# A hybrid SSM and attention layer on one core: both heads' scores in one PSUM tile of two banks

## The chip, the core and the metric

The kernel runs on one core of a Trainium2 chip. The metric is the device time of one launch in microseconds (us), as the median of the runs shown. TensorE is called PE here, VectorE DVE, ScalarE ACT, GpSimd POOL and SyncE SP, as in the profile.

## The reference, cut to what matters

One layer of a decoder with two branches, on 1024 prompt tokens and 32 sample tokens (8 sequences of 4), 1056 tokens in all. Both branches read one projection of the normalised input, and their gated sum and a feed-forward part are added to the stream:

```python
z = _rmsnorm(x, p['norm1_g']) @ p['w_in']
q, k, v, u, g = jnp.split(z, [o1, o2, o3, o4], axis=-1)     # q 512, k 128, v 128, u 512, g 2048
q = _rmsnorm(q.reshape(b, t, N_HEADS, HEAD_DIM), p['q_norm_g'])      # 8 heads of 64, 2 kv heads
k = _rmsnorm(k.reshape(b, t, N_KV_HEADS, HEAD_DIM), p['k_norm_g'])
attn, k_state, v_state = attn_fn(q, k, v, p['attn_sinks'])  # window of 128 keys, ALiBi, sinks
ssm, h_re, h_im = _s5_branch(u, h0_re, h0_im, p)            # scan over time, GELU, then y * sigmoid(y @ w_glu + b)
mixed = g_attn * (attn @ p['w_attn_o']) + g_ssm * (ssm @ p['w_ssm_o'])
x = x + mixed @ p['w_out']
hdn = jax.nn.relu(_rmsnorm(x, p['norm2_g']) @ p['w_up'])
x = x + (hdn * hdn) @ p['w_down']
```

## The kernel before

The activations lie with features on the partitions and the 1056 tokens along the free axis, cut into three chunks of 352 columns (c = 0, 1, 2). A dense product in fp32 is made of three fp32r matmuls (high part by high part, low by high, high by low: L131 to L133), each 128x128 by 352 columns. The weights come by DMA as `wraw` and are split into `whi` (ACT, L117) and `wlo` (DVE, L118).

The program runs in phases: the projection to `u`; the SSM in four quarters q (`stage0` to `stage3`), while PE takes the other projections (`z`) between; the norm of queries and keys; attention in eight blocks b of 128 queries, while PE takes the gates' projections (`z`) and then the GLU (`glu`) and the first of the output projections (`so`, `ao`) between; then the second phase with `so`, `ao`, `wo`, and last the feed-forward part, which the change doesn't reach. The order of instructions on each engine isn't written by hand: a scheduler lays it out from priorities, dependencies and free buffers, except where `in_turn` or `follow` adds an order. On the chip each engine takes its instructions in that order and waits at the first one that isn't ready.

PSUM has eight banks of 128x512 fp32, handed out by the tags `mm` (three), `sa` (two), `sb` (two) and `sc` (one). In the first phase `mmt`, `msa`, `msb` and `msc` give tiles of one bank each. With `msa` come: the first two chunks of the second tile of `u` (L329); the SSM's inputs `pv`, real and imaginary part, in two halves hb per quarter (L602), which four multiplications on DVE (L612 to L615) and two copies on ACT (L616, L617) read; the sums of squares of queries and keys (L726); the attention scores `sc` (L809); and the scores of the sample tokens `ssc` (L873). In the second phase `mmt2` (L972) goes through a cycle of seven tiles, of which the second and the sixth have the tag `sa`.

`attn_scores` makes the scores of a block in two parts mp of four matmuls: two query tiles m by two heads h. A head has 64 features, so a matmul uses one half of the rows (heads h = 1 and 0 use different halves), 128 queries by 256 keys (128 in block 0); head h writes to bank h. DVE adds the bias and takes the maximum out of PSUM (L820), ACT takes the exponential (L827), DVE scales (L835), PE transposes (`pt`, L841), ACT copies (`ptt`, L844), and PE makes the product with the values (`po`, L851). `sa_read` and `in_turn` give PE's scores an order: one after the other, and after the last read of the scores before.

The low parts of the squares of queries and keys, `qsl` (L731), come from the pool T2, of which three buffers exist, which the gates' tiles use as well. The tag `ptb` of the attention pool has two buffers of 128x1152, used only by the sample tokens, later.

The first products of the GLU read `a_hi` and `a_lo`, the split outputs `gr` of the SSM (`split`, L934: a cast on ACT, L935, and a subtraction on DVE, L936). `gemm_c` goes through the inputs k for one chunk; `gemm_k` goes through the chunks for one input, and so needs three banks at a time.

Of the kernel before, what the change touches and what calls it, by code (L numbers as in the profile page):

```python
# [23 lines left out]
CH = T // 3  # L24
# [34 lines left out]
def trunk_kernel(ctx, tc, xt, wts, wff, pp_d, cp_d, g1_d, abias, sbias, ckt, cvr, ck_tail, cv_tail,  # L59
# [142 lines left out]
    with ExitStack() as ph1:  # L202
# [3 lines left out]

        def msa(name):
            return pp1.tile([P, 512], F32, tag="sa", bufs=2, name=name)

# [3 lines left out]
        def msc(name):  # L213
            return pp1.tile([P, 512], F32, tag="sc", bufs=1, name=name)
# [70 lines left out]
        with phs:  # L285
# [42 lines left out]
            u0 = [mmt(f"u0_{c}") for c in range(3)]  # L328
            u1 = [msa("u1_0"), msa("u1_1"), msc("u1_2")]  # L329
            for k in range(8):  # L330
# [263 lines left out]
            def stage2(q, ut, s1o):  # L594
# [6 lines left out]
                for hb in range(2):  # L601
                    pv = [msa(f"pv{q}{hb}{ri}") for ri in range(2)]  # L602
                    for j in range(2):
# [121 lines left out]
        A.copy(bonr, C("bones"))  # L725
        pqs = [msa("qkss0"), msa("qkss1"), msc("qkss2")]  # L726
        for t_ in (4, 0, 1, 2, 3):
            z = kt if t_ == 4 else q4[:, t_, :]
            sq = newT(f"qsq{t_}")
            sqh = ap_.tile([P, 2048], F32R, tag="st", bufs=2, name=f"qsh{t_}")[:, :T]  # L730
            sql = newT2(f"qsl{t_}", F32R)  # L731
            A.activation(sq, z, AF.Square)
            A.copy(sqh, sq)
            V.tensor_sub(sql, sq, sqh.bitcast(F32))
            w = bonr[:, 8 - 2 * t_ : 18 - 2 * t_]
            for c in range(3):
                mm_(pqs[c][:10, :CH], w, sqh[:, chunks[c]], start=(t_ == 4), stop=False)
                mm_(pqs[c][:10, :CH], w, sql[:, chunks[c]], start=False, stop=(t_ == 3))
# [51 lines left out]
        def sink_terms(mx, sk, n, name):  # L790
# [5 lines left out]
            return nm, es  # L796
        sa_read = []


        def attn_scores(b):  # L800
# [6 lines left out]
            for mp in range(2):  # L807
                mms = []
                pst = [msa(f"sc{b}{mp}{h}") for h in range(2)]  # L809
                for m2 in range(2):  # L810
                    m = 2 * mp + m2
                    for h in (1, 0):
                        hs_ = slice(64 * h, 64 * h + 64)
                        mms.append(mm_(pst[h][:, m2 * 256 : m2 * 256 + nk], q4[hs_, m, b * P : b * P + P],
                                       kt[hs_, k0 : k0 + nk], start=True, stop=True))
                in_turn(mms, *sa_read)
                for m2 in range(2):
                    for h in range(2):
                        hd = 4 * h + 2 * mp + m2
                        rd = V.tensor_tensor_reduce(  # L820
                            st[:, hd, :nk], pst[h][:, m2 * 256 : m2 * 256 + nk], ab[:, hd, bo : bo + nk],
                            1.0, C("sink", hd, hd + 1), ALU.add, ALU.max, mx[:, hd : hd + 1],
                        )
                sa_read[:] = [rd.ins.name]
            nm, es = sink_terms(mx, C("sink"), NH, f"{b}")
# [30 lines left out]
        def attn_sample():  # L856
# [10 lines left out]
            mxs = [ap_.tile([P, 3], F32, tag="smx", bufs=2, name=f"smx{h}") for h in range(2)]  # L867
            ptbs = [ap_.tile([P, 9, P], F32, tag="ptb", bufs=2, name=f"ptb{h}") for h in range(2)]
            for h in range(2):
                nc.sync.dma_start(sbs[h], sbias[h])  # L870
            for c in range(3):
                s = chunks[c]
                pst = [msa(f"ssc{h}{c}") for h in range(2)]  # L873
                mms = []
                for h in (1, 0):
                    hs_ = halves[h]
                    mms.append(mm_(pst[h][:, :CH], qs[hs_, :, :].rearrange("p m t -> p (m t)"), kall[hs_, s],
                                   start=True, stop=True))
                in_turn(mms, *sa_read)
                for h in range(2):  # L880
                    mx = mxs[h]
                    rd = V.tensor_tensor_reduce(
                        ssts[h][:, s], pst[h][:, :CH], sbs[h][:, s], 1.0,
                        C("ssink", h, h + 1) if c == 0 else mx[:, c - 1 : c], ALU.add, ALU.max, mx[:, c : c + 1],
                    )
                sa_read[:] = [rd.ins.name]
            for h in range(2):
# [63 lines left out]
        for m in range(4):  # L951
# [3 lines left out]
            nc.sync.dma_start(gr, y_d[m])  # L955
            th = newT2(f"gth{m}")
            for c in range(3):
                ps = mmt(f"glu{m}_{c}")
                gemm_c([blk(wg, (m % 2) * 4 + k) for k in range(4)], aacts, ps, c)
                A.activation(th[:, chunks[c]], ps[:, :CH], AF.Tanh, bias=bh[:, 16 + m : 17 + m], scale=0.25)  # L960
# [7 lines left out]
    with ExitStack() as ph2:  # L968
        accp = ph2.enter_context(tc.tile_pool(name="accp", bufs=1))
        _mi = [0]  # L970

        def mmt2(name):  # L972
            i = _mi[0]
            _mi[0] += 1
            tag, n = (("mm", 3), ("sa", 2), ("mm", 3), ("sb", 2), ("mm", 3), ("sa", 2), ("sb", 2))[i % 7]
            return pp1.tile([P, 512], F32, tag=tag, bufs=n, name=name)

# [561 lines left out]
```

## Time and profile before

| what | us |
|---|---|
| three runs of the kernel before | 1361.0, 1364.49, 1365.66 |
| median | 1364.49 |
| the profiled execution | 1364.98 |
| its span, first to last instruction | 1363.2 |
| PE busy in it | 1311.4 (96%) |
| DVE, ACT, POOL busy | 906.5, 513.1, 484.8 |
| mean granted clock of PE | 0.987 |

A busy time of an engine is the time in which at least one of its instructions runs. A timeline gives for each instruction, or group of like ones in a row, its start, its duration and the idle time of its engine before it with what ended that; "x2" counts records, and a score in fp32 leaves two of them per matmul, a dense fp32r matmul one. Durations of PE's matmuls overlap, so what one costs is read from its start to the start of the next.

### The profile page before, as it was taken

What the parts mean: (1) busy time and instruction counts of PE and PEld (TensorE: products, weight loads), DVE (VectorE), ACT (ScalarE), POOL (GpSimd) and SP (SyncE); (2) the same over time, 40 slices, a digit from 0 to 9 for tenths busy, and PEclk for the clock granted to TensorE, in tenths of its full rate; (3) what the DMA queues carried; (4) which work ended last, traced back from release to release, by engine and by line L of the source; (5) the groups of instructions that cost most, each with busy time, mean ns of one, the idle gap of its engine ahead of it and who ended that gap; (6) DMA issues with size and microseconds to landing.
All of it is one profiled execution on the core that took longest, in us unless ns stands there. A gap on an engine that the chain in (4) does not pass through costs nothing.

```text
span 1363.2 us, 23526 instructions
## 1 busy us (share of the span) xinstructions
PE 1311.4 (96%) x9405; PEld 1250.7 (92%) x9405; DVE 906.5 (67%) x1383; ACT 513.1 (38%) x857; POOL 484.8 (36%) x356
## 2 busy tenths in 40 slices
PE   7988999999998999999999999999998999999998
PEld 6987999899876777999989999999998999999898
DVE  7859675534457856654686666566598595887973
ACT  5111233234147544223453444344365362533420
POOL 5495522000000000004344665675675332343630
PEclk9889999999998999999999999999999999999999
DMA  7233434463233313524233564444467382563621
GB/s 266 84 85 79 103 99 95 116 242 105 65 95 95 114 62 115 203 82 162 102 110 111 190 190 138 143 155 143 143 198 238 112 263 75 152 202 115 220 95 64
DMA packets 91789, 184.96 MB, mean 136 GB/s; under 512 B 23616, under 2 KB 32832, under 8 KB 91392
## 3 DMA queue, kind: packets, MB, share of 16 engines
q1 hardware_dynamic: 84768, 170.48, 39.6%
q10 hardware_dynamic: 6912, 12.98, 2.5%
q8 instruction: 74, 1.21, 0.4%
q14 instruction: 35, 0.29, 0.1%
HBM read 125.70 MB, written 57.56 MB: 134 GB/s over the span
## 4 chain that ended last, share of the span: by engine, by line
PE 74%; DVE 8%; DMA 3%; issue 2%; ACT 2%; POOL 1%; SPq 0%; DVEq 0%; POOLq 0%; ACTq 0%
PE X L1150 6%; PE X L1151 6%; PE X L1152 6%; PE C L1151 4%; PE z L131 4%; PE C L1150 4%; PE C L1152 4%; PE z L133 4%; PE z L132 4%; PE wo L131 2%; PE wo L132 2%; PE wo L133 2%; PE D L1151 2%; PE Y L1151 2%; PE D L1150 2%
## 5 line engine op out<-in xcount | busy, mean ns | idle before, releaser
L1150 PE MATMUL X<-slot_hi,fw 128*128 128x264 f32 x768 | 218.5, 285 | 2.0 <-ACT h L1169 0.9
L1151 PE MATMUL X<-slot_lo,fw 128*128 128x264 f32 x768 | 217.8, 284 | 0.4 <-DVE slot_lo L1076 0.4
L1152 PE MATMUL X<-slot_hi,fw 128*128 128x264 f32 x768 | 217.6, 283 | 0.0
L131 PE MATMUL z<-x_hi,whi 128*128 128x352 f32 x528 | 174.2, 330 | 1.8 <-DVE zt L268 1.8
L133 PE MATMUL z<-x_hi,wlo 128*128 128x352 f32 x528 | 172.9, 328 | 1.5 <-DVE wlo L118 1.5
L132 PE MATMUL z<-x_lo,whi 128*128 128x352 f32 x528 | 172.9, 328 | 0.0
L1012 DVE TENSOR_TENSOR fw<-f,fw 128x512 fp32r<-128x512 f32 x128 | 132.4, 1035 | 35.1 <-ACT fw L1011 35.1
L1150 PEld LDWEIGHTS X<-slot_hi,fw 128*128 128x128 f32 x768 | 144.6, 188 | 3.0 <-ACT h L1169 1.4
L1151 PEld LDWEIGHTS X<-slot_lo,fw 128*128 128x128 f32 x768 | 144.7, 188 | 0.6 <-DVE slot_lo L1076 0.6
L1152 PEld LDWEIGHTS X<-slot_hi,fw 128*128 128x128 f32 x768 | 144.1, 188 | 0.0
L1111 POOL TENSOR_TENSOR q<-x 128x528 f32<-128x528 f32 x4 | 5.7, 1432 | 374.2 <-DVE x L1102 374.2
L1011 ACT CAST fw<-f 128x512 fp32r<-128x512 f32 x128 | 79.2, 619 | 155.8 <-PE Y L1152 61.8
L997 POOL TENSOR_TENSOR f_s<-f,f 128x512 f32<-128x512 f32 x32 | 49.5, 1546 | 216.6 <-DMA f<-in_dram 176.2
L1012 DVE TENSOR_TENSOR fw<-f_s,fw 128x512 fp32r<-128x512 f32 x96 | 92.9, 969 | 38.3 <-ACT fw L1011 38.1
L133 PEld LDWEIGHTS z<-x_hi,wlo 128*128 128x128 f32 x528 | 100.0, 189 | 5.7 <-issue 3.6
L131 PEld LDWEIGHTS z<-x_hi,whi 128*128 128x128 f32 x528 | 100.6, 190 | 4.6 <-ACT whi L117 2.1
L132 PEld LDWEIGHTS z<-x_lo,whi 128*128 128x128 f32 x528 | 100.6, 191 | 2.0 <-issue 1.5
L117 ACT CAST whi<-wraw 128x1024 fp32r<-128x1024 f32 (+3 forms) x46 | 46.5, 1012 | 144.8 <-PE z L132 74.1
L1011 ACT CAST fw<-f_s 128x512 fp32r<-128x512 f32 x96 | 59.9, 624 | 90.0 <-PE C L1152 48.2
L1150 PE MATMUL Y<-slot_b,fw 128*128 128x264 f32 x256 | 73.3, 287 | 5.4 <-DVE y L1169 2.8
L1150 PE MATMUL C<-slot_b,fw 128*128 128x264 f32 x256 | 72.8, 285 | 0.9 <-ACT slot_b L1306 0.5
L1151 PE MATMUL C<-slot_b,fw 128*128 128x264 f32 x256 | 72.7, 284 | 0.9 <-DVE slot_b L1307 0.9
(364 smaller groups left out, 3838.0 us busy)
## 6 DMA issues: line engine op xcount, KB each, us to landing
f<-in_dram SPq DMA_DIRECT2D x128, 256.0 KB
st<-h_d SPq DMA_DIRECT2D x56, 528.0 KB
wraw<-in_dram SPq DMA_DIRECT2D x42, 512.0 KB
h_d<-h ACTq DMA_DIRECT2D x48, 264.0 KB
g_d<-gs SPq DMA_DIRECT2D x16, 528.0 KB
h_d<-hc SPq DMA_DIRECT2D x32, 264.0 KB
h_d<-hd SPq DMA_DIRECT2D x32, 264.0 KB
gr<-y_d SPq DMA_DIRECT2D x8, 528.0 KB
```

The lines of the kernel that those rows point to most:

```text
L117: A.copy(whi[:, s], raw[:, s])
L131: mm_(out, wh, ah[:, s], start=first, stop=False)
L132: mm_(out, wh, al[:, s], start=False, stop=False)
L133: mm_(out, wl, ah[:, s], start=False, stop=last)
L997: x = G.tensor_add(s1, a21, a22)
L1011: A.copy(w[:, 0], x)
L1012: V.tensor_sub(w[:, 1], x, w[:, 0].bitcast(F32))
L1111: G.tensor_add(t1, xa[:, :TH], xa[:, TH:])
L1150: mm_(o, wh, ah[:, j, s], start=start and j == 0, stop=False, **k)
L1151: mm_(o, wh, al[:, j, s], start=False, stop=False, **k)
L1152: mm_(o, wl, ah[:, j, s], start=False, stop=j == 3, **k)
```

## The change

There are three edits. First, `msa2` takes the place of `msa`: it gives one tile of two banks (tag `sa`, one buffer) and returns its two halves. All users of `sa` in the first phase take both banks at once, and the order by `sa_read` and `in_turn` is gone at the scores. In the second phase `mmt2` takes such a tile at every other call for `sa`, and gives out its second bank at the next. A tile of two banks can be taken again when both banks have been read. Second, `qsl` takes the buffers `ptb` of the attention pool. Third, the first tile of the GLU (m = 0) takes its three banks at once and goes through the inputs outermost (`gemm_k`); the other three go as before. Each engine has the same number of instructions as before; their order differs.

```diff
--- before.py
+++ after.py
@@ -204,8 +204,9 @@
         def mmt(name):
             return pp1.tile([P, 512], F32, tag="mm", name=name)
 
-        def msa(name):
-            return pp1.tile([P, 512], F32, tag="sa", bufs=2, name=name)
+        def msa2(name):
+            t = pp1.tile([P, 2, 512], F32, tag="sa", bufs=1, name=name)
+            return [t[:, i, :] for i in range(2)]
 
         def msb(name):
             return pp1.tile([P, 512], F32, tag="sb", bufs=2, name=name)
@@ -326,7 +327,7 @@
                 return un
 
             u0 = [mmt(f"u0_{c}") for c in range(3)]
-            u1 = [msa("u1_0"), msa("u1_1"), msc("u1_2")]
+            u1 = msa2("u1") + [msc("u1_2")]
             for k in range(8):
                 for ps, w in ((u0, w01[0]), (u1, w01[1])):
                     for c in range(3):
@@ -599,7 +600,7 @@
                 ga = sp.tile([P, 4, P], F32, tag="ga", name=f"ga{q}")
                 gb = sp.tile([P, 4, P], F32, tag="gb", name=f"gb{q}")
                 for hb in range(2):
-                    pv = [msa(f"pv{q}{hb}{ri}") for ri in range(2)]
+                    pv = msa2(f"pv{q}{hb}")
                     for j in range(2):
                         pj = 2 * hb + j
                         for ri in range(2):
@@ -723,12 +724,12 @@
         A.copy(selr, C("sel")[:10, :])
         bonr = ap_.tile([P, 18], F32R, name="bonr")
         A.copy(bonr, C("bones"))
-        pqs = [msa("qkss0"), msa("qkss1"), msc("qkss2")]
+        pqs = msa2("qkss") + [msc("qkss2")]
         for t_ in (4, 0, 1, 2, 3):
             z = kt if t_ == 4 else q4[:, t_, :]
             sq = newT(f"qsq{t_}")
             sqh = ap_.tile([P, 2048], F32R, tag="st", bufs=2, name=f"qsh{t_}")[:, :T]
-            sql = newT2(f"qsl{t_}", F32R)
+            sql = ap_.tile([P, 9 * P], F32R, tag="ptb", bufs=2, name=f"qsl{t_}")[:, :T]
             A.activation(sq, z, AF.Square)
             A.copy(sqh, sq)
             V.tensor_sub(sql, sq, sqh.bitcast(F32))
@@ -794,8 +795,6 @@
             V.tensor_add(es, sk, nm)
             A.activation(es, es, AF.Exp)
             return nm, es
-        sa_read = []
-
 
         def attn_scores(b):
             nk = 256 if b else 128
@@ -805,23 +804,20 @@
             mx = ap_.tile([P, NH], F32, tag="mx", bufs=2, name=f"mx{b}")
             ss = ap_.tile([P, NH], F32, tag="ss", bufs=2, name=f"ss{b}")
             for mp in range(2):
-                mms = []
-                pst = [msa(f"sc{b}{mp}{h}") for h in range(2)]
+                pst = msa2(f"sc{b}{mp}")
                 for m2 in range(2):
                     m = 2 * mp + m2
                     for h in (1, 0):
                         hs_ = slice(64 * h, 64 * h + 64)
-                        mms.append(mm_(pst[h][:, m2 * 256 : m2 * 256 + nk], q4[hs_, m, b * P : b * P + P],
-                                       kt[hs_, k0 : k0 + nk], start=True, stop=True))
-                in_turn(mms, *sa_read)
+                        mm_(pst[h][:, m2 * 256 : m2 * 256 + nk], q4[hs_, m, b * P : b * P + P],
+                            kt[hs_, k0 : k0 + nk], start=True, stop=True)
                 for m2 in range(2):
                     for h in range(2):
                         hd = 4 * h + 2 * mp + m2
-                        rd = V.tensor_tensor_reduce(
+                        V.tensor_tensor_reduce(
                             st[:, hd, :nk], pst[h][:, m2 * 256 : m2 * 256 + nk], ab[:, hd, bo : bo + nk],
                             1.0, C("sink", hd, hd + 1), ALU.add, ALU.max, mx[:, hd : hd + 1],
                         )
-                sa_read[:] = [rd.ins.name]
             nm, es = sink_terms(mx, C("sink"), NH, f"{b}")
             for hd in range(NH):
                 A.activation(st[:, hd, :nk], st[:, hd, :nk], AF.Exp, bias=nm[:, hd : hd + 1],
@@ -865,25 +861,23 @@
             sbs = [ap_.tile([P, T], F32, tag="sb", bufs=2, name=f"sb{h}") for h in range(2)]
             ssts = [newT(f"sst{h}") for h in range(2)]
             mxs = [ap_.tile([P, 3], F32, tag="smx", bufs=2, name=f"smx{h}") for h in range(2)]
-            ptbs = [ap_.tile([P, 9, P], F32, tag="ptb", bufs=2, name=f"ptb{h}") for h in range(2)]
+            ptbs = [ap_.tile([P, 9 * P], F32, tag="ptb", bufs=2, name=f"ptb{h}").rearrange("p (k t) -> p k t", t=P)
+                    for h in range(2)]
             for h in range(2):
                 nc.sync.dma_start(sbs[h], sbias[h])
             for c in range(3):
                 s = chunks[c]
-                pst = [msa(f"ssc{h}{c}") for h in range(2)]
-                mms = []
+                pst = msa2(f"ssc{c}")
                 for h in (1, 0):
                     hs_ = halves[h]
-                    mms.append(mm_(pst[h][:, :CH], qs[hs_, :, :].rearrange("p m t -> p (m t)"), kall[hs_, s],
-                                   start=True, stop=True))
-                in_turn(mms, *sa_read)
+                    mm_(pst[h][:, :CH], qs[hs_, :, :].rearrange("p m t -> p (m t)"), kall[hs_, s],
+                        start=True, stop=True)
                 for h in range(2):
                     mx = mxs[h]
-                    rd = V.tensor_tensor_reduce(
+                    V.tensor_tensor_reduce(
                         ssts[h][:, s], pst[h][:, :CH], sbs[h][:, s], 1.0,
                         C("ssink", h, h + 1) if c == 0 else mx[:, c - 1 : c], ALU.add, ALU.max, mx[:, c : c + 1],
                     )
-                sa_read[:] = [rd.ins.name]
             for h in range(2):
                 sst, mx, ptb = ssts[h], mxs[h], ptbs[h]
                 nm, es = sink_terms(mx[:, 2:3], C("ssink", h, h + 1), 1, f"s{h}")
@@ -954,9 +948,14 @@
             gr = newT2(f"gr2{m}")
             nc.sync.dma_start(gr, y_d[m])
             th = newT2(f"gth{m}")
+            gps = [mmt(f"glu{m}_{c}") for c in range(3)]
+            gw = [blk(wg, (m % 2) * 4 + k) for k in range(4)]
+            if m == 0:
+                gemm_k(gw, aacts, gps)
             for c in range(3):
-                ps = mmt(f"glu{m}_{c}")
-                gemm_c([blk(wg, (m % 2) * 4 + k) for k in range(4)], aacts, ps, c)
+                ps = gps[c]
+                if m:
+                    gemm_c(gw, aacts, ps, c)
                 A.activation(th[:, chunks[c]], ps[:, :CH], AF.Tanh, bias=bh[:, 16 + m : 17 + m], scale=0.25)
             V.scalar_tensor_tensor(nat(th), nat(th), 1.0, perm(gr), ALU.add, ALU.mult)
             V.scalar_tensor_tensor(th[:, SEQ:], th[:, SEQ:], 1.0, gr[:, SEQ:], ALU.add, ALU.mult)
@@ -968,11 +967,17 @@
     with ExitStack() as ph2:
         accp = ph2.enter_context(tc.tile_pool(name="accp", bufs=1))
         _mi = [0]
+        _sa = []
 
         def mmt2(name):
             i = _mi[0]
             _mi[0] += 1
             tag, n = (("mm", 3), ("sa", 2), ("mm", 3), ("sb", 2), ("mm", 3), ("sa", 2), ("sb", 2))[i % 7]
+            if tag == "sa":
+                if not _sa:
+                    t = pp1.tile([P, 2, 512], F32, tag="sa", bufs=1, name=name)
+                    _sa.extend(t[:, i, :] for i in range(2))
+                return _sa.pop(0)
             return pp1.tile([P, 512], F32, tag=tag, bufs=n, name=name)
 
         def mst2(name):
```

In the orders that follow, `sc` are scores, `ssc` scores of the sample tokens, `z` a gate's projection, `pt` transposes and `po` products of attention probabilities. Lines are those of each kernel (scores L814 before, L812 after; `ssc` L877 and L873; `pt` L841 and L837; `po` L851).

PE at the first part of the scores of block 2; before:

```order
2039 L131 MATMUL z_1_4270<-x_hi,whi_4239 128x352
2040 L814 MATMUL sc_3221<-kt,q_2860 128x256
2041 L132 MATMUL z_1_4270<-x_lo,whi_4239 128x352
2042 L133 MATMUL z_1_4270<-x_hi,wlo_4240 128x352
2043 L131 MATMUL z_1_4270<-x_hi,whi_4239 128x352
2044 L132 MATMUL z_1_4270<-x_lo,whi_4239 128x352
2045 L814 MATMUL sc_3220<-kt,q_2860 128x256
2046 L851 MATMUL po_3133<-ptt_3131,vtok 64x512
2047 L851 MATMUL po_3133<-ptt_3124,vtok 64x512
2048 L814 MATMUL sc_3221<-kt,q_2860 128x256
2049 L814 MATMUL sc_3220<-kt,q_2860 128x256
2050 L133 MATMUL z_1_4270<-x_hi,wlo_4240 128x352
```

After:

```order
2045 L133 MATMUL z_2_4267<-x_hi,wlo_4211 128x352
2046 L812 MATMUL sc_3206<-kt,q_2851 128x256 x4
2047 L131 MATMUL z_2_4267<-x_hi,whi_4210 128x352
2048 L132 MATMUL z_2_4267<-x_lo,whi_4210 128x352
```

The four scores were in three places, with gate matmuls and a product of probabilities between; they now stand in one.

PE at the first scores of the sample tokens, among the GLU's products; before:

```order
2211 L132 MATMUL glu_0_4463<-a_lo,whi_4455 128x352
2212 L133 MATMUL glu_0_4463<-a_hi,wlo_4456 128x352
2213 L877 MATMUL ssc_3431<-kall,qs 128x352
2214 L131 MATMUL glu_0_4463<-a_hi,whi_4455 128x352
2215 L132 MATMUL glu_0_4463<-a_lo,whi_4455 128x352
2216 L133 MATMUL glu_0_4463<-a_hi,wlo_4456 128x352
2217 L877 MATMUL ssc_3430<-kall,qs 128x352
2218 L131 MATMUL glu_0_4463<-a_hi,whi_4455 128x352
```

After:

```order
2184 L133 MATMUL glu_1_4435<-a_hi,wlo_4427 128x352
2185 L131 MATMUL glu_1_4435<-a_hi,whi_4426 128x352
2186 L873 MATMUL ssc_3410<-kall,qs 128x352 x2
2187 L837 MATMUL pt_3346<-cp,st_3281 128x128 x4
2188 L132 MATMUL glu_1_4435<-a_lo,whi_4426 128x352
2189 L133 MATMUL glu_1_4435<-a_hi,wlo_4427 128x352
2190 L131 MATMUL glu_2_4436<-a_hi,whi_4426 128x352
```

The two heads' scores were three dense matmuls apart; they now follow each other.

PE at the start of the GLU; before:

```order
2100 L841 MATMUL pt_3197<-cp,st_3137 128x128 x4
2101 L841 MATMUL pt_3204<-cp,st_3137 128x128 x4
2102 L814 MATMUL sc_3301<-kt,q_2860 128x256
2103 L814 MATMUL sc_3300<-kt,q_2860 128x256
2104 L814 MATMUL sc_3301<-kt,q_2860 128x256
2105 L814 MATMUL sc_3300<-kt,q_2860 128x256
2106 L131 MATMUL glu_0_4359<-a_hi,whi_4351 128x352
2107 L131 MATMUL glu_1_4373<-a_hi,whi_4351 128x352
2108 L131 MATMUL glu_2_4387<-a_hi,whi_4351 128x352
2109 L132 MATMUL glu_0_4359<-a_lo,whi_4351 128x352
```

After:

```order
2064 L812 MATMUL sc_3215<-kt,q_2851 128x256 x4
2065 L131 MATMUL glu_0_4330<-a_hi,whi_4322 128x352
2066 L131 MATMUL glu_1_4331<-a_hi,whi_4322 128x352
2067 L131 MATMUL glu_2_4332<-a_hi,whi_4322 128x352
2068 L837 MATMUL pt_3183<-cp,st_3125 128x128 x4
2069 L837 MATMUL pt_3190<-cp,st_3125 128x128 x4
2070 L132 MATMUL glu_0_4330<-a_lo,whi_4322 128x352
```

The transposes of block 1's second 128 keys (`pt`, two banks of four) stood ahead of the last scores before the GLU, which were the first part of block 3; in the new order they stand behind three products of the GLU's first input, and the last scores before the GLU are the second part of block 2.

## Rows read from the trace of the kernel before

**Rows 1.** The page, part 1: busy time by engine, share of the span, instructions.

```profile
PE 1311.4 (96%) x9405; PEld 1250.7 (92%) x9405; DVE 906.5 (67%) x1383; ACT 513.1 (38%) x857; POOL 484.8 (36%) x356
```

**Rows 2.** Stages: stretch and its length, busy time by engine, PE clock, DMA share.

```profile
50.00:265.00 215.00, 199.38 (x1303) 189.30 (x1302) 151.96 (x259) 45.50 (x78) 98.99 (x114) 0.97 0.36 95
265.00:415.00 150.00, 150.00 (x905) 133.75 (x904) 64.40 (x157) 50.57 (x86) 0.00 (x0) 1.00 0.36 123
415.00:436.00 21.00, 16.95 (x76) 10.64 (x75) 16.40 (x44) 19.61 (x48) 0.00 (x0) 0.84 0.40 128
436.00:500.00 64.00, 64.00 (x391) 50.52 (x389) 45.03 (x122) 32.55 (x76) 0.00 (x0) 1.00 0.34 102
500.00:531.00 31.00, 25.24 (x140) 16.78 (x139) 17.87 (x60) 17.12 (x48) 0.00 (x0) 0.94 0.00 1
531.00:690.00 159.00, 158.68 (x996) 158.22 (x994) 93.37 (x146) 49.00 (x82) 33.67 (x28) 1.00 0.42 142
```

**Rows 3.** Waits of PE by what was waited for: total, times, longest.

```profile
PE py L649 <- DVE ht L635: 2.8, 3, 1.6
...
PE py L651 <- DMA tm<-krep: 2.1, 1, 2.1
```

**Rows 4.** Timeline of PE, 388 to 392 us: start, duration, instruction, records.

```profile
388.64 0.70 PE L814 MATMUL sc<-kt,q 64*128 64x256 f32 x2
389.26 0.42 PE L133 MATMUL z<-x_hi,wlo 128*128 128x352 f32 x1
389.62 1.13 PE L814 MATMUL sc<-kt,q 64*128 64x256 f32 x6
390.68 0.43 PE L131 MATMUL z<-x_hi,whi 128*128 128x352 f32 x1
390.94 0.32 PE L132 MATMUL z<-x_lo,whi 128*128 128x352 f32 x1
391.10 0.32 PE L133 MATMUL z<-x_hi,wlo 128*128 128x352 f32 x1
```

**Rows 5.** Timeline of PE: scores of both heads in one run.

```profile
363.02 0.49 PE L814 MATMUL sc<-kt,q 64*128 64x128 f32 x4
363.44 0.43 PE L132 MATMUL z<-x_lo,whi 128*128 128x352 f32 x1
...
395.96 0.70 PE L814 MATMUL sc<-kt,q 64*128 64x256 f32 x4
396.60 0.66 PE L841 MATMUL pt<-cp,st 128*128 128x128 f32 x4
```

**Rows 6.** Timeline of PE, 410 to 413 us: transposes among gate matmuls.

```profile
410.20 0.38 PE L841 MATMUL pt<-cp,st 128*128 128x128 f32 x2
...
412.16 1.13 PE L814 MATMUL sc<-kt,q 64*128 64x256 f32 x6
```

**Rows 7.** Timeline of PE, 456 to 458 us: a score of the sample tokens.

```profile
456.60 0.86 PE L877 MATMUL ssc<-kall,qs 64*128 64x352 f32 x2
457.38 0.43 PE L132 MATMUL glu<-a_lo,whi 128*128 128x352 f32 x1
```

**Rows 8.** Timeline of ScalarE at the start of the GLU.

```profile
415.32 4.10 ACT L935 CAST a_hi<-gr 128x1024 fp32r<-128x1024 f32 x4
419.32 0.58 ACT L844 COPY ptt<-pt 128x512 f32<-128x512 f32 x1
```

**Rows 9.** Timeline of PE at the end of attention, 507 to 522 us.

```profile
507.19 1.14 PE L814 MATMUL sc<-kt,q 64*128 64x256 f32 x8
510.12 0.43 PE L131 MATMUL ao<-a_hi,whi 128*128 128x352 f32 x1 [1.80 <-ACT a_hi L935]
...
519.86 1.94 PE L851 MATMUL po<-ptt,vtok 128*64 128x512 f32 x8 [2.46 <-ACT ptt L844]
```

**Rows 10.** Groups of instructions of VectorE: count, busy, mean ns, idle before.

```profile
L1037 DVE SCALAR_TENSOR_TENSOR ta<-ta,ao 128x352 f32<-128x352 f32 x24 | 12.5, 519 | 16.0 <-PE ao L133 16.0
...
L612 DVE TENSOR_TENSOR gr<-pv,ctab 128x256 f32<-128x256 f32 x8 | 3.3, 418 | 13.3 <-PE pv L608 8.2 <-POOL ctab L560 5.1
```

## The prediction

> **What bounds the kernel now.** I read the page's busy times first, then the stages, then the waits of TensorE (PE), then PE's timeline around the instructions that the diff touches. PE is busy 96% of the span [rows 1], and no other engine comes near it. The stages [rows 2] show where the rest lies: 265 to 415 us (queries, keys, gates, first blocks of attention) has no idle time on PE at all; the start of the GLU, 415 to 436, has 4.05; the end of attention, 500 to 531, has 5.8; 531 to 690 has 0.3; the SSM, 50 to 265, has 15.6. So the time goes down if PE's own instructions take less, or if waits in those three places shrink. Work on another engine that ends sooner counts only there. In the SSM the waits that the change can reach are those for ht and tm, 2.8 and 2.1 [rows 3].
>
> PE is busy, but not always at its best. A dense matmul of 352 columns starts 0.16 us after the one before it (390.94 to 391.10) [rows 4]. A single score matmul holds PE for 0.62 (388.64 to 389.26), three in a row for 1.06 (389.62 to 390.68) [rows 4]; each matmul is two records. A dense one behind scores takes 0.26, and one that stands between two runs of scores takes 0.36, so going in and coming out cost 0.10 each [rows 4]. Two scores of the two heads, on the two halves of the rows, are no dearer than one: 395.96 to 396.60 is 0.64 [rows 5]. Four have the same duration as three [rows 4, 9]. So a run of one or two scores costs 0.62 + 0.20 = 0.82, and one of three or four 1.06 + 0.20 = 1.26. What counts is how many runs there are, not how many scores.
>
> That price belongs to half-height matmuls alone. Between 410.20 and the scores that start at 412.16 eight 128x128 transposes stand among six dense matmuls, in single pieces [rows 6]; after 0.10 for going into the scores, 1.86 us remain: 0.96 for six dense ones, and 0.11 for each transpose, with nothing left for the changes between them. The Trainium skill, "TensorEngine Tiling (Array Packing)", section Key Properties, has the rule behind it: a change of the array's tiling mode drains TensorE. The trace agrees (0.10 at each side of scores, none at transposes).
>
> **The change part by part.**
>
> *Scores.* Before, each head's bank becomes free by itself, and the order in which PE takes the scores was laid down while one bank was free and the other not: head 1, some dense work, head 0, and so on. As one tile, both banks come free together, and the order shows the heads side by side. I counted the runs in both programs. Before, block 0 (128 keys) has 4 pairs; after, 6 runs. One costs 0.42 + 0.20 = 0.62 (363.02 to 363.44) [rows 5]: 2.5 becomes 3.7, +1.2. Blocks 1 to 7: before, 11 short and 12 long runs, 9.0 + 15.1 = 24.1; after, 4 short and 13 long, 3.3 + 16.4 = 19.7: **-4.4**. Sample scores: before, 6 single ones, 0.78 + 0.20 each (456.60 to 457.38) [rows 7] = 5.9; after, 3 pairs. A pair of these isn't in the trace; the nearest row is the pair of scores, as dear as one [rows 5], so 2.9 and **-3.0**; if it were twice one, -0.6, for the changes saved alone. Sum of the runs: -6.2 (-3.8 with dear pairs). It all lies on PE, in stretches without idle time or nearly so, and so on the path.
>
> *Waits at the GLU's start* [rows 2, 8]. ScalarE makes four casts of 1.0 us for the first two inputs in one stretch of 4.10, and the copies of the transposed probabilities stand behind them (419.32). In the new order the second half of block 1's transposes comes between the first inputs' products and the next ones, and needs a bank that such a copy frees: a wait of some 2 us, where before there were 4.05 in all. I also find products of the third input fed a little sooner. PE's clock in this stretch is 0.84 of full [rows 2], at the lower of its two levels (1.2 of 2.4 GHz) for 0.16 x 21 x 2 = 6.7 us, after the waits; that costs 3.4 of PE's time. If that stays, the stage is even; if the shorter waits spare it, -2; if waits of 2 us are added to those of before, +2. I take -0.3, since casts and copies on ScalarE are the same work. gemm_k itself brings nothing: the products stood in the order of the inputs before (three glu products of the first input in a row), it only writes that down.
>
> *The tail of attention* [rows 2, 9]. Block 7's last scores stand behind the same number of dense matmuls in both (2136), so the chain from there (reduce, exponentials, scaling, transposes, copies, product) is as long. But block 6's last scores stand 32 and block 7's first 15 dense matmuls earlier, so VectorE and ScalarE reach the last scores with less in hand, and block 6's product comes 11 earlier. Waits of 1.80 before the first attention products and of 2.46 before a product of probabilities [rows 9] are what this can shorten. Bounds: nothing (the freed PE time is waited away), and all of the 5.8 idle [rows 2]. I walked PE, VectorE and ScalarE through the new order by the durations of before and take **-2.5**.
>
> *The second phase.* The two banks are handed out by turns, and a new pair must wait until both have been read. Mostly two banks' worth of products (12 to 24 of 0.16) lie between; once, the third chunk of the fourth SSM output tile stands directly behind the products of the pair before, and waits for VectorE's read of 0.52 [rows 10] and the lag: **+0.7**. No wait gives 0; three such 2.1.
>
> *SSM.* The second half of a quarter's inputs (pv) must now wait for all six readers of the first, four multiplications of 0.41 [rows 10] and two small copies, where before each bank waited for its own. The order puts 30 or more rows between them, about 5 us. The last two quarters stand 10 to 40 dense matmuls later, since work before them was moved up; that lengthens the time for ht and tm, which PE waited for [rows 3], but also shortens what follows. I take 0, with -2 and +3.
>
> *Squares' low parts and u.* The low parts move to two buffers of another pool, from three. The stretch has no idle PE [rows 2], and this cover is large: 0; without it a square's subtraction late by one buffer would cost about 1. The first chunks of u are one tile: at most one dense matmul more, 0.2, taken as 0.
>
> Sum: -6.2 - 0.3 - 2.5 + 0.7 = -8.3. The profiled execution took 1364.98, the median of the three runs is 1364.49, half a microsecond less: **1356**.
>
> **The rivals.** *No change (within 4.1 us, 0.3%, about what a measurement can tell):* PE gets through its runs sooner and waits for the same chains. For it: the tail ends in a chain that isn't shorter, and casts set the GLU's start. Against it: 265 to 415 has no wait, and 436 to 500 none either, so sooner there is sooner at the next wait, unless that is a DMA's. If only half of the -6.2 lasts and the tail gives nothing: 1364.5 - 3.1 + 0.7 = 1362. That pairs of sample scores cost double, with nothing from the tail, gives 1361.
>
> *Slower:* the tile of two banks as a lock in the SSM. In-order PE stands at the second pv until VectorE is through with the first; behind it are queued the dense products and py. It decides when VectorE starts its four multiplications over 3 us after the first pv. Per half it costs up to 4 x 0.41 + 0.35 = 2.0, four times 8, and with a wait for tm or ht as before, 2.1 or 1.6 [rows 3], again in two quarters, about 12: 1364.5 - 8.3 + 12 = 1368. For it: VectorE is busy there for 152 of 215 us [rows 2]. Against: the 30 rows between. The Trainium skill, "PSUM — Partial Sum Buffer", section PSUM bank collisions raise a hardware error, advises to guard PSUM by bank; this change guards two as one. No row of before shows what that costs.
>
> *The change doesn't do what it says:* four short runs remain in blocks 1 to 7 and block 0 is more broken than before; the counts are of the program, so this is in the sum.
>
> **How the numbers follow.** Forecast (1352 to 1360): 0.66. Within 0.3%: 0.24. Slower by more: 0.10, at 1368 mostly. Low end: -6.2, the tail's 5.8, -2 and -2 in GLU and SSM: 1349. High end: dear pairs (-3.8), tail nothing, +0.7, +2 and +1 of the SSM's: 1364.
>
> **What would show it.** The runs: L873 three pairs of 0.8 each; single scores in blocks 1 to 7 at most four; PE's busy time about 6 less. Idle of PE in 500 to 531's stretch 3 or so; its waits for pt at the GLU's start 2. It would be wrong if PE's idle time in the SSM is over 18, if a pair of sample scores takes 1.5, or if PE's clock is at the lower level in further stretches.

## The result, and the profile after

The changed kernel takes 1354.12 us (median of five runs, 1352.64 to 1357.15), the kernel before 1364.49. The ratio is 0.9929, with a 95% interval of 0.9916 to 0.9941: 8 to 11.5 us less. The profiled execution after took 1352.64; that of before 1364.98. They lie 12.3 apart, 2 us more than the medians, so what follows from these two traces is on the large side. The page after, span and busy times by engine, beside [rows 1]:

```profile
span 1350.8 us, 23514 instructions
...
PE 1302.6 (96%) x9405; PEld 1249.6 (93%) x9405; DVE 901.4 (67%) x1383; ACT 512.4 (38%) x857; POOL 484.2 (36%) x356
```

PE is still busy 96% of the span, and 8.8 us less than before. To see where, I cut both traces at the same amount of work: at dense matmul 240 and 1180 (most of the SSM), 1690 and 2160 (attention and what stands between it), and within that 1872 to 1908 (the GLU's start) and 2010 to 2160 (the tail). The times at which these stand differ, the dense work between them doesn't; PE's other work in them is the same too, but at the GLU's start, which holds eight transposes more after. Before, by the view of busy time in stretches (stretch, its length, busy time and count of PE, PE's weight loads, DVE, ACT and POOL, then PE's granted clock, DMA share and GB/s):

```profile
59.50:271.00 211.50, 195.88 (x1286) 186.10 (x1285) 146.92 (x235) 47.27 (x79) 94.37 (x98) 0.97 0.38 101
365.70:528.40 162.70, 152.98 (x866) 115.05 (x865) 103.57 (x314) 83.94 (x216) 0.00 (x0) 0.97 0.25 77
417.30:437.30 20.00, 16.87 (x77) 11.15 (x77) 16.18 (x45) 18.56 (x49) 0.00 (x0) 0.83 0.45 140
466.60:528.40 61.80, 56.12 (x350) 42.43 (x348) 37.41 (x122) 30.60 (x84) 0.00 (x0) 0.97 0.23 70
```

After, the same four:

```profile
59.50:266.80 207.30, 193.91 (x1287) 185.21 (x1286) 142.97 (x235) 45.63 (x78) 92.53 (x98) 0.98 0.40 101
362.00:515.00 153.00, 145.09 (x866) 113.41 (x865) 104.39 (x315) 84.43 (x216) 0.00 (x0) 0.98 0.26 82
409.10:428.70 19.60, 16.66 (x85) 12.94 (x86) 16.45 (x44) 16.04 (x35) 0.00 (x0) 0.83 0.48 142
457.40:515.00 57.60, 53.51 (x350) 40.97 (x348) 38.56 (x124) 30.93 (x84) 0.00 (x0) 1.00 0.23 76
```

The SSM takes 207.3 in place of 211.5. Attention takes 153.0 in place of 162.7: PE is busy 7.9 less, and its idle time (length less busy) falls from 9.7 to 7.9. The GLU's start is 0.4 shorter, with its eight transposes more, and the tail 4.2: there PE is idle 4.1 in place of 5.7, and its granted clock is 1.00 in place of 0.97. Behind dense matmul 2160 the two traces go alike but for about a microsecond in the second phase; the cut at the first feed-forward matmul shows 12.4 us between them, the end 12.3.

The scores, by the timeline of PE after (start, duration, instruction, records; two records are a matmul):

```profile
430.69 1.13 PE L812 MATMUL sc<-kt,q 64*128 64x256 f32 x8
431.75 0.43 PE L131 MATMUL glu<-a_hi,whi 128*128 128x352 f32 x1
...
437.38 0.70 PE L812 MATMUL sc<-kt,q 64*128 64x256 f32 x4
438.01 0.44 PE L837 MATMUL pt<-cp,st 128*128 128x128 f32 x2
...
445.12 0.86 PE L873 MATMUL ssc<-kall,qs 64*128 64x352 f32 x4
445.91 0.66 PE L837 MATMUL pt<-cp,st 128*128 128x128 f32 x4
```

A run of four lasts from 430.69 to 431.75, 1.06; a pair on two halves 0.63; and a pair of the sample tokens' scores 0.79 (445.12 to 445.91), as much as one of them before [rows 7]. The groups of scores, before and after (busy, mean ns):

```profile
L814 PE MATMUL sc<-kt,q 64*128 64x256 f32 (+1 forms) x128 | 24.2, 407 | 0.0
...
L877 PE MATMUL ssc<-kall,qs 64*128 64x352 f32 x12 | 5.1, 508 | 0.0
```

```profile
L812 PE MATMUL sc<-kt,q 64*128 64x256 f32 (+1 forms) x128 | 20.5, 395 | 0.2 <-DVE mx L817 0.2
...
L873 PE MATMUL ssc<-kall,qs 64*128 64x352 f32 x12 | 2.6, 508 | 0.0
```

Busy time of scores falls by 3.7, of sample scores by 2.5, and there are 7 runs fewer (33 before, 26 after), with 0.20 more at each for the changes of the array's height. A part of the 3.7 is the clock's, as at the GLU's start before, where the granted clock is 0.83:

```profile
421.65 1.22 PE L814 MATMUL sc<-kt,q 64*128 64x256 f32 x2
422.80 3.68 PE L851 MATMUL po<-ptt,vtok 128*64 128x512 f32 x8
```

A single score takes 1.15 there (421.65 to 422.80), in place of 0.62 [rows 4].

The waits at the GLU's start, in the tail, and the one in the second phase, by the timeline of PE after:

```profile
409.13 0.75 PE L131 MATMUL glu<-a_hi,whi 128*128 128x352 f32 x3 [0.84 <-ACT a_hi L929]
411.73 1.97 PE L837 MATMUL pt<-cp,st 128*128 128x128 f32 x8 [1.85 <-ACT ptt L840]
...
427.18 0.43 PE L132 MATMUL glu<-a_lo,whi 128*128 128x352 f32 x1 [0.82 <-DVE a_lo L930]
...
507.34 2.52 PE L837 MATMUL pt<-cp,st 128*128 128x128 f32 x12 [1.96 <-DVE st L831]
510.54 0.66 PE L837 MATMUL pt<-cp,st 128*128 128x128 f32 x4 [0.68 <-ACT ptt L840]
...
525.86 0.43 PE L131 MATMUL so<-a_hi,whi 128*128 128x352 f32 x1 [0.61 <-DVE ta L1042]
```

At the GLU's start PE waits 0.84 for the first cast, 1.85 for the copy that stands behind the casts, and 0.82 for a low part. In the tail it waits 1.96 for block 7's scaled probabilities and 0.68 for a copy; the rest of its 4.1 goes to other copies. At 525.86 it waits 0.61 for VectorE's read of a product; with the two banks as two tiles again this wait is gone (e5).

### The profile page after: what moved, and what is told of

The parts are those of the page before. It is cut to its first block, busy times and chain, and to the rows that moved or that the text cites. A ratio compares the mean times of both kernels' runs of the same rounds, so it can differ in the third digit from the quotient of the medians.

```text
span 1350.8 us, 23514 instructions
## 1 busy us (share of the span) xinstructions
PE 1302.6 (96%) x9405; PEld 1249.6 (93%) x9405; DVE 901.4 (67%) x1383; ACT 512.4 (38%) x857; POOL 484.2 (36%) x356
## 4 chain that ended last, share of the span: by engine, by line
PE 76%; DVE 13%; issue 3%; DMA 3%; POOL 2%; ACT 1%; SPq 1%; DVEq 0%; POOLq 0%; ACTq 0%
PE X L1155 6%; PE X L1156 6%; PE X L1157 6%; PE z L133 4%; PE z L131 4%; PE z L132 4%; PE C L1156 4%; PE C L1155 4%; PE C L1157 4%; PE wo L131 2%; PE wo L132 2%; PE wo L133 2%; PE D L1156 2%; PE D L1155 2%; PE D L1157 2%
```

## The experiments

e1 to e6 and e11 are the kernel before or after with parts of the edits taken or left; e7 to e10 have something of their own besides. So that tiles of one and of two banks can both be had, the tag `sa` has a pool of its own in them, closed and opened again behind the SSM and ahead of the second phase (in e11 behind `u` too). No run has that pool alone. As far as the traces show, it moves nothing on PE: up to the end of the SSM e1 has the order of the kernel before, from dense matmul 1690 on e3 has it, and e6 has that of the changed kernel but for three matmuls. "Dense matmul N" counts PE's dense products from the start. A ratio is to the kernel before, run beside each; in brackets stands its 95% interval. Idle time is that of PE, length less busy.

**Scores alone (e1).** The kernel before with

```diff
-        pqs = [msa("qkss0"), msa("qkss1"), msc("qkss2")]
+        pqs = msa2("qkss") + [msc("qkss2")]
...
-                pst = [msa(f"sc{b}{mp}{h}") for h in range(2)]
+                pst = msa2(f"sc{b}{mp}")
...
-                pst = [msa(f"ssc{h}{c}") for h in range(2)]
+                pst = msa2(f"ssc{c}")
```

and without `in_turn` there. Expected:

> The kernel before, with two banks in one tile for the scores of attention, the sample scores and the sums of squares alone; squares' low parts, u, pv, GLU and second phase as before. In the order all runs of scores are whole: 4 pairs in block 0, 12 runs of four and one of eight, 3 pairs of sample scores. Theory of runs (a run of one or two scores costs 0.62 and 0.20 for its two changes of array height, one of three or four 1.06 and 0.20): 32.5 us before, 21.8 here, so 10 to 11 less, near 1354, and the SSM as before. Rival, waits: the time saved on runs is waited away at the GLU's start and behind block 7's scores, which end at the same dense matmul as before; 1361 or more.

Measured: 1360.06, ratio 0.9966 (0.9955 to 0.9978), 3 to 6 us less, half of what the runs alone say. The stretch from 1690 to 2160, and the wait of PE's scores in it:

```profile
364.80:520.90 156.10, 143.47 (x866) 112.08 (x865) 103.35 (x314) 84.59 (x216) 0.00 (x0) 0.98 0.25 80
410.80:436.10 25.30, 19.63 (x108) 13.25 (x108) 19.35 (x63) 20.83 (x53) 0.00 (x0) 0.93 0.41 129
...
PE sc L824 <- DVE mx L829: 3.4, 3, 1.8
```

Busy time falls by 9.5, of it 1.7 because PE ran 3.4 us less at its lower clock. The runs alone promise 10 to 11, or some 0.9 less, since the sum counts the run of eight like one of four. But idle time rises from 9.7 to 12.6, nearly all of it at the GLU's start, dense matmuls 1872 to 1908 (5.7 in place of 3.1), and not in the tail (5.9 in place of 5.7), where the rival had it too. Scores wait 3.4 us for `mx`, DVE's last read of the two banks: with both banks in one tile, and five parts of scores between dense matmuls 1872 and 1908, the next part finds the tile not yet read. Neither theory was right alone: the runs are worth their price on PE, and a part of that is waited away.

**Squares alone (e2).** The kernel before with

```diff
-            sql = newT2(f"qsl{t_}", F32R)
+            sql = ap_.tile([P, 9 * P], F32R, tag="ptb", bufs=2, name=f"qsl{t_}")[:, :T]
```

> The kernel before, with the squares' low parts in the attention pool's buffers alone. PE has no idle time there, so by the prediction it costs nothing where it stands. But the order of the scores moves with it: 19 single ones in blocks 1 to 7 instead of 9, 37.2 us of runs instead of 32.5. Theory of runs: 4 to 5 us slower, near 1369. Rival (the runs are no price, only waits count): within 2 us of before. A third outcome: block 7's scores come 15 dense matmuls earlier here, and if that counts more than the runs, faster than before.

Measured: 1364.11, ratio 1.0006 (0.9997 to 1.0016), no difference.

```profile
364.40:526.70 162.30, 155.72 (x864) 115.85 (x862) 103.33 (x314) 84.12 (x216) 0.00 (x0) 0.98 0.24 77
```

PE is busy 2.7 more, by the runs that are in more pieces (4.7) less some lower clock, and idle 6.6 in place of 9.7. So this edit isn't a matter of buffers: it moves the order of all scores, cuts them up, and brings the first part of block 7 from dense matmul 2136 to 2121. Loss and gain cancel: the rival's time came true, but not by its reason, since the runs had their price.

**The SSM's tiles alone (e3, e11).** The kernel before with

```diff
-            u1 = [msa("u1_0"), msa("u1_1"), msc("u1_2")]
+            u1 = msa2("u1") + [msc("u1_2")]
...
-                    pv = [msa(f"pv{q}{hb}{ri}") for ri in range(2)]
+                    pv = msa2(f"pv{q}{hb}")
```

(e11: the second of them alone).

> The kernel before, with two banks in one tile for u and pv alone; all scores in the order of before. The trace after is 4.2 us ahead at the end of the SSM, 2.2 of it less waiting and up to 1.7 less time at PE's lower clock. If that is this edit's doing: 1360 (3 to 5 less), idle time of PE in 50 to 265 us near 13.4. If it comes from something else in the change or from chance in the clock: 1363 to 1366, idle 15 to 17.

> The kernel before, with two banks in one tile for pv alone; u as before. e3, with both, was 3.0 faster than before. u's part changes 43 rows of PE at the very start, all else in the SSM's order is pv's. If the gain is pv's: 1361 to 1362, waits of PE over dense matmuls 240 to 1180 near 13.3 (15.6 before). If it was u's: 1364.

Measured: e3 1361.35, ratio 0.9976 (0.9965 to 0.9987); e11 1360.54, ratio 0.9977 (0.9964 to 0.9990). Both are 1.4 to 5 us faster; e11 has the whole of it without u, so the gain is pv's. The SSM, dense matmul 240 to 1180, in e3:

```profile
58.90:267.90 209.00, 195.66 (x1286) 185.92 (x1285) 142.22 (x235) 45.57 (x78) 92.48 (x98) 0.97 0.41 101
```

and in e11:

```profile
58.90:266.00 207.10, 193.87 (x1286) 185.17 (x1285) 142.98 (x235) 45.52 (x78) 92.54 (x98) 0.98 0.40 102
```

and in e1, which leaves pv as it was:

```profile
58.90:270.00 211.10, 195.15 (x1286) 185.13 (x1285) 147.13 (x235) 47.39 (x79) 94.92 (x98) 0.98 0.38 101
```

Idle time is 13.3 and 13.2, as after (13.4), against 15.6 before and 16.0 in e1. It is so in every trace: the ten with pv's tile of two banks take 206.5 to 209.0 us for this stretch and are idle 12.1 to 14.3, the three without (before, e1, e2) 211.1 to 211.5 and 15.2 to 16.0. Of the 4.2 between the two profiled executions 2.2 are idle time and some 1.7 the clock, which isn't the edit's: PE ran about 13.7 us at its lower clock in this stretch before and 10.2 after, but 13.7 in e3 as well, and 10.2 in e1. The waits of PE in the SSM that are gone or smaller, before, beside those for ht and tm [rows 3]:

```profile
PE wtp L540 <- DVE wri L532: 3.5, 2, 3.3
...
PE wtp L540 <- DVE wri L535: 2.6, 2, 1.6
...
PE z L131 <- DVE zt L268: 1.8, 1, 1.8
```

After:

```profile
PE wtp L541 <- DVE wri L533: 3.3, 1, 3.3
PE py L650 <- DVE ht L636: 3.1, 2, 2.3
PE pk L587 <- POOL wout L575: 2.9, 2, 2.3
PE z L133 <- DVE wlo L118: 2.0, 1, 2.0
PE wtp L541 <- DVE wri L536: 0.9, 1, 0.9
PE py L652 <- DMA tm<-krep: 0.9, 1, 0.9
```

The order of e11's SSM and of the changed kernel's is the same but for the start. A wait of 1.8 for a read of a gate's tile is gone, those for `wri` fall from 6.1 to 4.2, the one for tm from 2.1 to 0.9, and idle time before the products `py` that waits for nothing in the profile from 1.2 to 0.2; a new one of 2.9 for POOL's `wout` stands against that. The fall for `wri` is in part chance: it is 4.8 in e1, with the old order, and 5.3 in e3. None is a wait of pv for its tile. What the runs show is that the edit's order waits less; that it does so is not the purpose of a tile of two banks, but what the scheduler made of it.

**All but the squares (e4).** The changed kernel with the squares' line as before.

> The changed kernel with the squares' low parts where they were before. Its scores stand as in e1: 21.8 us of runs against 26.3 in the changed kernel. Theory of runs: 4 to 5 us faster than the changed kernel, near 1350. Rival: the scores of block 7 stand together behind dense matmul 2136, where the changed kernel has the first part 15 earlier, and the longer chain at the tail of attention (two reduces of four, 8 exponentials at 0.5) gives it back: 1354.

Measured: 1359.03, ratio 0.9952 (0.9938 to 0.9966), some 3 us slower than the changed kernel by the ratios, 5 by the medians; the intervals just meet.

```profile
360.60:517.20 156.60, 143.35 (x868) 111.36 (x866) 103.54 (x314) 84.62 (x216) 0.00 (x0) 0.98 0.25 80
...
PE sc L824 <- DVE mx L829: 3.4, 3, 1.8
```

It has the shortest busy time of all in this stretch, 143.4, and the longest waits but one, 13.2, with the same 3.4 for `mx`. The theory of runs, which expected 1350, falls, and the rival's 1354 is 5 short. It had named the tail, where idle time is 6.2 in place of 4.1 in the changed kernel; but the GLU's start has 6.0 in place of 2.9 besides. By these traces the squares' edit, which costs runs, is worth its price beside the scores' edit, since with it the parts of scores stand further apart.

**Second phase (e5) and GLU (e6).** The changed kernel with `mmt2`, or the GLU's loop, as before.

> The changed kernel with the two banks of the second phase as two tiles again; all else as changed. The trace after has one wait there that before doesn't have, 0.61 to 0.70 us, and is 1.0 later over dense matmuls 2160 to 2900. If that wait is the pair's: 0.7 to 1.0 less than the changed kernel, some 1353.3, and no wait of that kind in the trace. If the time returns as a wait behind it: no difference.

> The changed kernel with the first GLU tile's inputs written innermost again, as before. Only three matmuls of the whole program stand in another place, so the prediction's price of nothing should hold: 1354, within 1 us of the changed kernel. A difference of over 2 us would say that the inputs' order is worth something after all.

Measured: e5 1352.99, ratio 0.9918 (0.9900 to 0.9936); e6 1354.41, ratio 0.9929 (0.9911 to 0.9948). The wait of 0.61 isn't in e5's trace, and its second phase is 1.0 shorter (dense matmul 2160 to 2900). All four traces with the pair there take 119.5 to 119.6 us for it, the nine without 118.5. As a time that is within the intervals, so e5 isn't shown to be the faster. The GLU's edit is worth nothing that can be measured. Attention and tail of e5, then the tail of e6:

```profile
360.90:515.30 154.40, 146.49 (x868) 114.84 (x866) 104.36 (x315) 84.31 (x216) 0.00 (x0) 0.97 0.25 81
455.20:515.30 60.10, 56.00 (x351) 43.39 (x349) 38.55 (x124) 30.92 (x84) 0.00 (x0) 0.94 0.23 73
```

```profile
455.90:516.20 60.30, 56.20 (x351) 43.38 (x349) 38.58 (x124) 30.91 (x84) 0.00 (x0) 0.94 0.23 73
```

Both tails are in the changed kernel's order and have its waits, but PE's clock is 0.94 there, where the profiled execution after had 1.00, and they take 60.1 and 60.3 us in place of 57.6. So 2.5 us of the tail's gain in that one execution aren't the order's. At the GLU's start it is the other way: 18.4 us at 0.91 in both, 19.6 at 0.83 after.

**Where the scores stand (e7, e9, e10).** e7 is e5 with `tc.high_priority(offset=300)` around `attn_scores(b + 1)`; e10 the same without the squares' edit; e9 is e5 with one order more:

```diff
+                        if b == 7 and mp == 0:
+                            follow(x_, *last_pt)
```

where `x_` is the score and `last_pt` the transpose of the block before that PE takes last.

> As e5 (second phase with two tiles), and the scores of every block with a higher priority. Runs of scores: 23.0 us, where the changed kernel has 26.3; block 6's last part stands at dense matmul 2122 (2097 in the changed kernel), and both parts of block 7 at 2136 (2121 and 2136). Theory of runs alone: 3.3 less than e5, near 1350. Theory that the place of block 7's first part and the bunching of scores at the GLU's start decide as much: waits of PE from dense matmul 1690 to 2160 grow from 7.9 us to 11 or more, and the time is that of e5 or up to 3 above.

> As e5, with one order more: block 7's first four scores stand behind block 6's transposes, so at dense matmul 2136 in place of 2121; 38 of 9111 rows of PE are in another place, runs and dense products are the same. Theory of the tail (VectorE's and ScalarE's work on block 7 starts 15 dense matmuls later and PE waits for it): waits from 2010 to 2160 grow from 4.1 us by 2 to 3, time 1355 to 1356 against 1353 for e5. If the place of block 7's first part isn't what counts: as e5.

> As e4 (squares' low parts where they were), with the second phase's two tiles and a higher priority for every block's scores: 23.1 us of runs, the scores of blocks 2 to 4 still between dense matmuls 1868 and 1937, but block 5 at 2030 and 2046 as in the changed kernel, block 6 at 2052 and 2134, block 7 twice at 2136. Waits from 1690 to 2160 were 9.7 us before, 7.9 in the changed kernel, 13.2 in e4. If whole runs are worth what PE's rows say and only the bunching at the GLU's start is bad: waits 10 or less, time near 1353. If late blocks 6 and 7 are as bad: 12 or more, 1356 to 1358.

Measured: e7 1355.50, ratio 0.9940 (0.9921 to 0.9958); e9 1357.64, ratio 0.9946 (0.9933 to 0.9958); e10 1358.39, ratio 0.9950 (0.9935 to 0.9964). They are 2.5, 4.7 and 5.4 us slower than e5 by the medians, 3.0, 3.8 and 4.4 by the ratios. The intervals of e5 and e7 overlap, those of e9 and e10 just meet e5's (0.9900 to 0.9936), so what sets them apart is read from the traces. e7, 1690 to 2160:

```profile
362.60:521.20 158.60, 145.30 (x867) 113.02 (x866) 103.98 (x315) 83.56 (x216) 0.00 (x0) 0.96 0.25 79
...
PE sc L824 <- DVE mx L829: 4.7, 4, 1.8
```

e9, the tail:

```profile
457.20:519.30 62.10, 56.56 (x350) 43.96 (x348) 38.99 (x124) 30.93 (x84) 0.00 (x0) 0.92 0.22 70
...
PE pt L853 <- DVE st L847: 2.5, 2, 1.9
PE ao L131 <- DVE mx L833: 1.9, 1, 1.9
```

e10, 1690 to 2160:

```profile
360.60:520.20 159.60, 147.63 (x868) 113.23 (x866) 103.21 (x314) 84.07 (x216) 0.00 (x0) 0.96 0.25 78
```

e7 has 3.3 us less of runs than e5 by their price, and waits 13.3 in place of 7.9, of it 4.7 for `mx`: 2.6 more at the GLU's start and 2.8 more in the tail. Its second theory held. e10 waits 12.0, also in both places (5.5 and 5.5, in e5 2.9 and 4.1), though scores wait little for `mx` there. So it doesn't tell what bunching costs from what late blocks cost. In e9 nothing but 38 rows' places differ: block 7's first scores 15 dense matmuls later make the waits of the tail 5.5 in place of 4.1, and PE's clock there falls to 0.92. That theory held in kind; its size for waits was 1.4, not 2 to 3, and the tail is 2.0 longer with the clock. The profiled executions of e9 and e5 are 5.9 apart, and the other 3.9 lie in stretches whose order is the same in both, so most of what parts these two executions isn't this edit's.

**Order of the halves (e8).** The changed kernel with the loops over m and h exchanged, so that a part's scores come as head 1, 1, 0, 0.

```diff
-                for m2 in range(2):
-                    m = 2 * mp + m2
-                    for h in (1, 0):
+                for h in (1, 0):
+                    for m2 in range(2):
+                        m = 2 * mp + m2
```

> The changed kernel with the four scores of a part in the order head 1, 1, 0, 0 in place of 1, 0, 1, 0, so that only the two in the middle use different halves of the rows side by side. If two scores on the two halves run together (0.64 for two in the trace before): a run of four lasts three steps of 0.53, 1.6 in place of 1.06, so 6 to 7 us more for the 13 whole runs, less 1 for two runs fewer in block 0: near 1360 if nothing hides it. If the halves don't run together and only changes of height are dear: 1.06 as before, time 1353 to 1354.

Measured: 1355.57, ratio 0.9933 (0.9914 to 0.9952), as the changed kernel. From its timeline:

```profile
428.94 1.14 PE L824 MATMUL sc<-kt,q 64*128 64x256 f32 x8
430.01 0.43 PE L131 MATMUL glu<-a_hi,whi 128*128 128x352 f32 x1
...
435.64 1.13 PE L824 MATMUL sc<-kt,q 64*128 64x256 f32 x4
436.69 0.44 PE L849 MATMUL pt<-cp,st 128*128 128x128 f32 x2
```

A run of four still takes 1.07 (428.94 to 430.01), so the 1.6 that I expected was wrong, and that run told the theories apart only at one place: at 435.64 a pair of the same head takes 1.05, where a pair of both heads took 0.63 after. So the halves do run side by side. From its start to the next instruction's a run takes about 0.43 for each score on the half that has more, and 0.2 once (0.63 for one, 1.06 for two); the 0.20 for the changes of height comes on top. PE doesn't hold the second half's scores back behind the first's.

## Why the prediction was right, and where it wasn't

The forecast was 1356, with 1349 to 1364; 1354.12 was measured, 10.4 us less than before where 8.3 was said. The mechanism for attention was right. One term, the SSM's, was wrong, and without its 3 us the kernel would stand near 1357: that the sum came within 2 us is in part luck.

- **Runs of scores, -6.2: right.** Pairs of sample scores are as dear as one, and every kind of run has the price that was said. PE's busy time from dense matmul 1690 to 2160 fell by 7.9. Of that 1.7 is the clock (3.4 us less at the lower level), and 0.5 came back just ahead of 1690, where two single scores of block 0 stand after for one pair before: 5.7 remain.
- **The GLU's start, -0.3: right.** Idle time fell from 3.1 to 2.9, the wait for the copy behind the casts was 1.85 (some 2 said), and the clock was at its lower level as before (0.83).
- **The tail, -2.5: right in kind, too large.** The term was one of waits, and idle time there fell from 5.7 to 4.1 (some 3 said), by 1.6, in e5 and e6 as well. The rest of the 4.2 is runs (six in place of eight in this stretch), which the first term counts, and the clock. e9 shows that the place of block 7's first part is a cause, worth 1.4 of waits.
- **Second phase, +0.7: right by the trace.** One wait of 0.61, and 1.0 over the stretch with what follows.
- **SSM, 0 with -2 to +3: wrong.** It's 4.2 in the trace, 2.2 of it idle time, and 3.2 by the ratios of e3 and e11, a third of the whole gain. The step that failed: I priced what a tile of two banks can make pv wait for, and the later quarters, and took what the new order gives back as no more than that. The lock of pv's second half, the main rival, doesn't occur: no wait of PE after is for pv's tile. That the order around the four quarters would meet fewer of its waits (15.6 to 13.4) wasn't looked for; a walk of wri, zt and tm through the new order, as was done for the tail, was the way to look.
- **Squares, 0: right as a price, wrong as a description.** No wait came from two buffers. But alone the edit moves every score behind it, at +4.7 of runs and -3.1 of waits (e2), and by the trace the changed kernel without it waits 5.3 more (e4). The prediction counted runs in the order with all edits, so the sum had this in it unseen. That also is why "whole runs are good" doesn't carry further: e1, e4 and e7 have fewer runs, and wait more.
- **gemm_k, 0: right** (e6).

With the measured sizes the sum is -5.7 - 0.2 - 1.6 + 1.0 - 3.2 = -9.7, as the ratio says (0.9929); each size is read from one trace or two ratios, so a nearness to the tenth means nothing.

That half-height work costs 0.10 at each change is in line with the Trainium skill, "TensorEngine Tiling (Array Packing)", section Key Properties (a change of tiling mode drains TensorE). The same section says that different tiles can execute in parallel; the traces agree (two scores on one half take 1.05 in e8, two on two halves 0.63 after).

Three things stay open. The mechanism by which the squares' two buffers, and pv's tile, move the order lies in the scheduler and wasn't followed. e4's distance to the changed kernel is at the edge of what the runs tell. And what e7, e9 and e10 lose to e5 is shown as waits in their traces, hardly as a time.

## What to carry to other kernels

Price short matmuls of another array height by the run and not by the piece, from start to start in the timeline; then ask in which order they come, since scores that are made early and together wait for the reads of their bank, and scores that are made late leave PE waiting for the softmax behind them. An edit of buffers that a scheduler sees is an edit of the order of everything behind it: compare orders edit by edit, and cut both traces at equal work.

## What the runs showed of the hardware

Two fp32 matmuls on different halves of the rows run side by side in either order of issue, so that four in the order 1, 1, 0, 0 take 1.07 us, as long as two on one half alone (1.05). And with the same order and the same waits PE's clock falls in one execution and not in another: it is 1.00 in the tail after and 0.94 in e5 and e6, which take 2.5 us more for it.
